# The second head's operands move over by one block, so that the states and the removed values of both heads lie on a diagonal and one masked VectorE operation keeps them

## The chip, the cores and the metric

The kernel runs on one core of a Trainium2 chip. Five engines take part: TensorE (PE, its weight loads shown apart as PEld), VectorE (DVE), ScalarE (ACT), GpSimd (POOL) and SyncE (SP), which only issues transfers here. Each engine works through its own instructions in the order in which they stand; semaphores hold an instruction until what it needs is there. The metric is device time in microseconds (us), the median of several runs of one program; lower is better.

## The reference, cut to what matters

One decoder layer: an RMSNorm, one input projection, then 16 heads of RWKV-7 time mixing beside 16 heads of dilated window attention, an output projection and a last RMSNorm. The change lies in the time mixing, whose recurrence is, per head with a 64x64 state:

```
def step(state, inp):
    r_t, w_t, k_t, v_t, av_t, bv_t = inp              # av = -kk, bv = kk * a
    sa = jnp.einsum('bhvk,bhk->bhv', state, av_t)     # the value that is removed
    state = (state * w_t[:, :, None, :] + sa[..., None] * bv_t[:, :, None, :]
             + v_t[..., None] * k_t[:, :, None, :])
    return state, jnp.einsum('bhvk,bhk->bhv', state, r_t)
```

SEQ is 1024, the head size 64. All tensors are float32.

## The kernel before

**Units and slots.** The recurrence is computed in blocks of C = 64 steps. Two heads (a pair) share the 128 partitions, one in rows 0 to 63 and one in rows 64 to 127. A unit is one pair and one half of the sequence, so there are 16 units of NC_ = 8 blocks. `rwkv` goes over the units; at each unit it lays the work of four units at different stages into 24 slots: the chain of this unit, `finish` of the one before, `late` and `invert` of the next, `prepare` and `products` of the one after that. Behind the events of a slot it sends 4 matmuls of the input projection (128x512, from `proj_steps`, L179) to TensorE as filler. A scheduler that runs when the program is built may shift instructions a little on each engine, so the built order is what counts.

**The chain** (`chain`, three slots a block, called a step here) is serial. `first`: z = AR·Sd + MV·Vd on TensorE, where Sd [128, 2, 64] holds both heads' states as a block diagonal; `spread` (L704, L705) copies z into zd, again as a block diagonal, DVE the first head's half and ACT the second's. `second`: z = U·zd on TensorE gives the removed values; `spread` (L707 on DVE, L708 on ACT) scales them by rn (DVE) and rn1 (ACT) and writes ud. `third`: T = MV·Vd + AR·Sd + TU·ud; rows 0 to 63 of T are the new states of both heads side by side, rows 64 to 127 their outputs; `spread` scales the states by dec and writes the next Sd. All chain matmuls stand on L693 (`mm`). `heads_out` (L745, ACT) copies the outputs of four blocks from T to Y.

**What feeds the chain.** `prepare` builds AR (three 64-column blocks: identity, receptance, removal key), BK and rn on DVE, with dec on POOL (L435) and ACT (L436) and rn1 on ACT (L464). `products` multiplies AR by BK (pa, L559), masks the result into TU on DVE (L566) and copies it to MV on ACT (L569), where a POOL affine_select (L570) clears the future. `invert` builds U, the inverse of a triangular matrix, with column steps and transposes on DVE, small matmuls on PE and a trip through DRAM. `late` adds the turned keys to TU and MV and the values to Vd.

**Behind the time mixing** the same TensorE queue goes on with the attention and the output projection, which the change does not touch.

Of the kernel before, what the change touches and what calls it, by code (L numbers as in the profile page):

```python
# [45 lines left out]
class Kern:  # L46
# [237 lines left out]
    def rwkv(self, pairs=range(NPAIR), apairs=range(NPAIR)):  # L284
        nc = self.nc
        with ExitStack() as ctx:
# [99 lines left out]
    def prepare(self, d):  # L386
# [66 lines left out]
        def norm():  # L453
# [9 lines left out]
            d["rn1"] = self.mid.tile([64, NC_], F32, name="rn1", bufs=3)  # L463
            S.copy(out=d["rn1"], in_=rn[64:128])  # L464
# [17 lines left out]
        def receptance():  # L482
            V.tensor_tensor(out=self.c192(d["AR"])[:, :, 1], in0=c3(d["rs"]), in1=d["W"][:, :, 1:C + 1], op=ALU.mult)
# [10 lines left out]
    def late(self, d):  # L494
# [28 lines left out]
        def keys2(c4):  # L523
            tq, cs = t["tq"], slice(c4 * 4, c4 * 4 + 4)
            for e in range(2):
                er = slice(e * 64, e * 64 + 64)
                S.copy(out=d["TU"][er, cs, 0], in_=tq[0:64, :, e])
                S.copy(out=self.c192(d["MV"])[er, cs, 0], in_=tq[64:128, :, e])
# [14 lines left out]
    def products(self, d):  # L543
        nc = self.nc
        V, S, G = nc.vector, nc.scalar, nc.gpsimd
        er = [slice(0, 64), slice(64, 128)]

        def step(c4):
# [14 lines left out]
        def step2(c4):  # L563
            cs, q = slice(c4 * 4, c4 * 4 + 4), d["pq"]
            for e in (1, 0):
                V.tensor_tensor(out=d["TU"][er[e], cs, 1:3].rearrange("p c a t -> p c (a t)"), in0=q[e][0:64],  # L566
                                in1=bc(self.mask[0:64, 1].unsqueeze(1), (64, 4, 128)), op=ALU.mult)
                f = self.c192(d["MV"])[er[e], cs, 1:3].rearrange("p c a t -> p c (a t)")
                S.copy(out=f, in_=q[e][64:128])  # L569
                G.affine_select(out=f, in_=f, pattern=[[0, 4], [-1, 2], [1, 64]], compare_op=ALU.is_ge, fill=0.0, base=0,  # L570
                                channel_multiplier=-1)
# [18 lines left out]
    def invert(self, d, U):  # L590
# [17 lines left out]
        def clear():  # L608
            G.memset(U[:, 0:NC_], 0.0)

        def back():
            ud = self.dpool.tile([4, 16, 16, 16], F32, name="ud")
            nc.sync.dma_start(out=ud.rearrange("b q s t -> (b q) (s t)"), in_=d["UB"])
            for e in range(2):
                for b in range(4):
                    r = e * 64 + b * 16
                    nc.sync.dma_start(out=U[r:r + 16, 0:NC_, b * 16:b * 16 + 16],
# [6 lines left out]
        def m0():  # L624
            t["UT"] = self.tmp("vr2", "UT", (128, NC_, C))
            t["Xs"] = self.inv.tile([128, NC_, 32], F32, name="Xs")
            V.transpose(out=fl(t["UT"]), in_=fl(U[:, 0:NC_]))

        def m1():
            xq = t["xq"] = self.ps_tr.tile([128, NC_, 16], F32, name="xq", tag="tr")  # L630
            for c in range(NC_):
                for g in range(4):
                    b = 32 * (g % 2)
                    nc.tensor.matmul(xq[hs(g), c], lhsT=t["LT"][rs(g), c, b:b + 16], rhs=U[rs(g), c, b + 16:b + 32], start=True,
# [6 lines left out]
        def m2():  # L641
            dq = t["dq"] = self.ps_tr.tile([128, NC_, 16], F32, name="dq", tag="tr")
            for c in range(NC_):
                for g in range(4):
                    b = 32 * (g % 2)
                    nc.tensor.matmul(dq[hs(g), c], lhsT=t["UT"][hs(g), c, b:b + 16], rhs=t["Xs"][hs(g), c, 0:16], start=True,
                                     stop=True, skip_group_check=True)

        def m2c():
            for g in range(4):  # L650
                b = 32 * (g % 2)
                S.copy(out=U[hs(g), 0:NC_, b + 16:b + 32], in_=t["dq"][hs(g)])
# [6 lines left out]
        def m3():  # L659
            x2 = t["x2"] = self.ps_tr.tile([128, NC_, 32], F32, name="x2", tag="tr")  # L660
            for c in range(NC_):
                for e in range(2):
                    nc.tensor.matmul(x2[hi[e], c], lhsT=d["TU"][lo[e], c, 2, 32:64], rhs=t["UT"][lo[e], c, 0:32], start=True,
# [20 lines left out]
    def chain(self, d, nxt):  # L684

# [15 lines left out]
        def spread(out, q, scale):  # L701

            if scale is None:
                V.tensor_copy(out=out[er[0], 0], in_=q[0:64, 0:64])  # L704
                S.copy(out=out[er[1], 1], in_=q[0:64, 64:128])  # L705
            else:
                V.tensor_scalar(out=out[er[0], 0], in0=q[0:64, 0:64], scalar1=scale[0], scalar2=None, op0=ALU.mult)  # L707
                S.activation(out=out[er[1], 1], in_=q[0:64, 64:128], func=AF.Copy, scale=scale[1])  # L708

        def first(c):  # L710
# [7 lines left out]
            spread(zd, t["z"][:, 0], None)  # L718
# [3 lines left out]
        def second(c):  # L722
            mm(t["z"][0:66, 1], f2(d["U"])[:, c * 64:c * 64 + 66], self.zds[c % 2], True, True)
            spread(self.uds[c % 2], t["z"][:, 1], [d["rn"][0:64, c:c + 1], d["rn1"][:, c:c + 1]])

        def third(c):
# [8 lines left out]
            spread(self.Sds[(c + 1) % 2], T, [dec[:, e, n:n + 1] for e in range(2)])  # L735
# [4 lines left out]
    def heads_out(self, d, c4):  # L740
# [3 lines left out]
        for e in range(2):  # L744
            self.nc.scalar.copy(out=d["Y"][e * 64:e * 64 + 64, 4 * c4:4 * c4 + 4], in_=d["T", c4][64:128, :, e * 64:e * 64 + 64])  # L745
# [418 lines left out]
```

## Time and profile before

| what | value |
|---|---|
| median of 3 runs | 1553.68 us (1553.39 to 1553.86) |
| profiled execution, its own time | 1555.3 us |
| its span, first to last instruction | 1553.6 us |
| mean granted TensorE clock over the span | 0.998 of full speed (2.4 GHz) |
| matmul instructions | 10721 |
| chain of the first unit starts, chain of the last ends | about 114 us, about 842 us |

The profiled execution is one run with the hardware profiler on. A busy time is the sum over an engine's instructions without overlaps. Matmuls are pipelined: one 128x512 matmul is shown as about 0.40 us long while the next starts 0.23 us after it, so that a short wait of TensorE hides in the tail of the matmul ahead of it and the busy share of PE looks better than it is. "Idle before" is the time in which an engine had nothing running just before an instruction, and the arrow names what ended it.

### The profile page before, as it was taken

To read this page: it belongs to the slowest core of one execution; us is meant where nothing else is said; L and a number is where in the kernel's file an instruction comes from. 1 tells how busy PE (TensorE), PEld (TensorE's weight loads), DVE (VectorE), ACT (ScalarE), POOL (GpSimd) and SP (SyncE) were. 2 spreads that over 40 slices of the span, in tenths; PEclk is the share of its full clock that TensorE was granted. 3 is DMA by queue.
4 is the path that set the end of the run, shared out by engine and by line. 5 is a ranking of instruction groups with operands and counts; after the bars stand their busy time and mean duration, and the time that the engine had idled before them with its cause. 6 is when DMAs were issued, how large, how long until landed. Compare 5 with 4: busy or idle time off the path is not lost.

```text
span 1553.6 us, 29135 instructions
## 1 busy us (share of the span) xinstructions
PE 1486.1 (96%) x10721; PEld 1201.3 (77%) x10721; DVE 1009.3 (65%) x2776; ACT 897.6 (58%) x2080; POOL 442.0 (28%) x563
## 2 busy tenths in 40 slices
PE   5999999999999999999999999999999999899997
PEld 4877777777777777777777788888888888787886
DVE  6866776667776677766743557667676666956144
ACT  6655666666676666666643556555565565655221
POOL 3211111111111121112211534334443343456442
PEclk9999999999999999999999999999999999999999
DMA  6321111111111111111111201111111111426452
GB/s 199 90 48 33 41 40 39 41 34 40 47 32 41 47 33 41 39 38 41 34 39 34 70 28 42 35 35 34 38 52 34 36 55 55 159 92 203 142 161 99
DMA packets 178829, 94.87 MB, mean 61 GB/s; under 512 B 58413, under 2 KB 164606, under 8 KB 178686
## 3 DMA queue, kind: packets, MB, share of 16 engines
q1 hardware_dynamic: 174942, 86.19, 19.4%
q10 hardware_dynamic: 3744, 6.82, 1.3%
q8 instruction: 84, 1.38, 0.4%
q14 instruction: 59, 0.48, 0.1%
HBM read 75.01 MB, written 17.83 MB: 60 GB/s over the span
## 4 chain that ended last, share of the span: by engine, by line
PE 60%; DVE 17%; ACT 16%; issue 3%; DMA 2%; POOL 1%; SPq 0%; DVEq 0%; ACTq 0%; POOLq 0%
PE pq L179 28%; PE oq L1048 10%; PE o L994 3%; PE z L693 3%; PE T L693 3%; PE mp L921 2%; PE sp L954 2%; ACT Y L745 1%; DVE I L422 1%; ACT MV L569 1%; PE sp L974 1%; ACT Vd L513 1%; DVE TB L604 1%; ACT shtmp L213 1%; PE pa L559 1%
## 5 line engine op out<-in xcount | busy, mean ns | idle before, releaser
L179 PE MATMUL pq<-xh,wh 128*128 128x512 f32 x1040 | 429.1, 413 | 0.0
L179 PE MATMUL pq<-xl,wh 128*128 128x512 f32 x1040 | 412.3, 396 | 0.0
L179 PE MATMUL pq<-xh,wl 128*128 128x512 f32 x1040 | 303.3, 409 | 0.0
L179 PEld LDWEIGHTS pq<-xh,wh 128*128 128x128 f32 x1040 | 195.9, 188 | 32.6 <-ACT xh L157 0.3
L179 PEld LDWEIGHTS pq<-xl,wh 128*128 128x128 f32 x1040 | 196.4, 189 | 30.9 <-DVE xl L158 0.4
L179 PEld LDWEIGHTS pq<-xh,wl 128*128 128x128 f32 x1040 | 184.5, 189 | 31.9
L1048 PE MATMUL oq<-ow,qr 128*128 128x512 f32 x512 | 161.9, 394 | 1.2 <-ACT ow L1029 0.6
L982 POOL TENSOR_TENSOR pl<-p,ph 128x512 fp32r<-128x512 f32 (+2 forms) x96 | 102.3, 1072 | 202.2 <-ACT ph L981 182.4
L923 DVE CUSTOM_DVE_ANT_0 mp<-mp,maskq 128x512 f32<-128x512 f32 (+1 forms) x192 | 105.5, 570 | 68.4 <-PE mp L921 59.9
L977 ACT ACTIVATE p<-p 128x512 f32<-128x512 f32 (+2 forms) x144 | 64.6, 452 | 104.2 <-DVE p L976 103.3
L171 POOL TENSOR_TENSOR wl<-wraw,wh 128x512 fp32r<-128x512 f32 x64 | 85.5, 1354 | 110.4 <-PE pq L179 58.4
L1043 POOL TENSOR_TENSOR vr<-kr,qr 128x512 fp32r<-128x512 f32 (+2 forms) x68 | 90.8, 1340 | 80.5 <-ACT qr L1042 70.0
L1048 PEld LDWEIGHTS oq<-ow,qr 128*128 128x128 f32 x512 | 95.9, 188 | 22.8 <-ACT ow L1029 1.1
L1048 PE MATMUL oq<-ow,vr 128*128 128x512 f32 x256 | 101.2, 395 | 1.9 <-POOL vr L1043 1.9
L170 ACT CAST wh<-wraw 128x512 fp32r<-128x512 f32 x138 | 80.7, 616 | 28.6 <-PE pq L179 23.4
L1042 ACT CAST qr<-kr 128x512 fp32r<-128x512 f32 (+2 forms) x68 | 40.2, 594 | 93.5 <-PE oq L1048 52.0
L976 DVE TENSOR_TENSOR p<-sp,maskt 128x512 f32<-128x512 f32 (+2 forms) x144 | 65.2, 457 | 43.3 <-PE sp L974 41.9
L570 POOL TENSOR_SCALAR_AFFINE_SELECT MV<-MV 64x512 f32<-64x512 f32 x64 | 47.8, 747 | 125.2 <-ACT MV L569 114.2
L708 ACT ACTIVATE ud<-z,rn 64x64 f32<-64x64 f32 x128 | 39.3, 307 | 65.3 <-DVE ud L707 63.6
L707 DVE TENSOR_SCALAR ud<-z,rn 64x64 f32<-64x64 f32 x128 | 34.3, 268 | 58.1 <-PE z L693 57.9
L693 PEld LDWEIGHTS T<-ud,TU 128*128 128x128 f32 x256 | 42.5, 188 | 34.8 <-ACT ud L708 28.2
L708 ACT ACTIVATE Sd<-T,dec 64x64 f32<-64x64 f32 x120 | 36.9, 307 | 53.5 <-DVE Sd L707 52.0
(236 smaller groups left out, 3158.4 us busy)
## 6 DMA issues: line engine op xcount, KB each, us to landing
wraw<-in_w_in_dram SPq DMA_DIRECT2D x138, 256.0 KB
kr<-mixd SPq DMA_DIRECT2D x60, 256.0 KB
oraw<-in_w_out_dram SPq DMA_DIRECT2D x16, 512.0 KB
xt<-in_x_dram SPq DMA_DIRECT2D x8, 512.0 KB
ld<-TU SPq DMA_DIRECT2D x32, 128.0 KB
mixd<-zt SPq DMA_DIRECT2D x16, 256.0 KB
mixd<-gt SPq DMA_DIRECT2D x16, 256.0 KB
xr<-in_x_dram ACTq DMA_DIRECT2D x16, 256.0 KB
```

What stands on the lines that cost most here:

```text
L170: nc.scalar.copy(out=wh[:, ks], in_=raw)
L171: eng.tensor_tensor(out=wl[:, ks], in0=raw, in1=wh[:, ks].bitcast(F32), op=ALU.subtract)
L179: return [lambda i=i, a=a, b=b: self.nc.tensor.matmul(q, lhsT=a, rhs=b, start=(i == 0), stop=(i == len(ops) - 1)) for i, (a, b) in enumera ...
L570: G.affine_select(out=f, in_=f, pattern=[[0, 4], [-1, 2], [1, 64]], compare_op=ALU.is_ge, fill=0.0, base=0, channel_multiplier=-1)
L693: mm = lambda out, w, x, start, stop: nc.tensor.matmul(out, lhsT=w, rhs=f2(x), start=start, stop=stop, skip_group_check=True)
L708: S.activation(out=out[er[1], 1], in_=q[0:64, 64:128], func=AF.Copy, scale=scale[1])
L923: V.tensor_tensor_reduce(out=mp[:, :kn], in0=mp[:, :kn], in1=self.maskq[:, v0:v0 + kn], op0=ALU.add, op1=ALU.max, scale=1.0, scalar=-3e38, ...
L976: V.tensor_tensor(out=p[:, :qn], in0=sp[:, :qn], in1=self.maskt[:, u0:u0 + qn], op=ALU.add)
L977: S.activation(out=p[:, :qn], in_=p[:, :qn], func=AF.Exp)
L982: G.tensor_tensor(out=pl[:, :qn], in0=p[:, :qn], in1=ph[:, :qn].bitcast(F32), op=ALU.subtract)
L1043: nc.gpsimd.tensor_tensor(out=ml, in0=raw, in1=mh.bitcast(F32), op=ALU.subtract)
L1048: nc.tensor.matmul(q, lhsT=m[:, i], rhs=v, start=(k == 0 and j == 0), stop=(k == 15 and j == 2))
```

## The change: what it does, and the diff

For the second head (rows 64 to 127) the blocks of the operands stand one block further or in another order. AR holds [receptance, identity, removal key] there in place of [identity, receptance, removal key], and TU and MV are laid out likewise (`ra` lists the two blocks that `products` writes: 1 and 2 for the first head, 0 and 2 for the second). U stands one block to the right, so U is cleared and transposed over 9 blocks. With that, T and the second z carry the first head's states or removed values in rows 0 to 63 and columns 0 to 63, and the second head's in rows 64 to 127 and columns 64 to 127; what lies off the diagonal is outputs or of no use. `spread` becomes one DVE operation over 128x128: (q times a per-row scale) times the 0/1 block mask `bd`. The first z keeps its two copies. dec becomes one [128, 8] tile written by POOL; rn1 goes. The receptance is written by two half-height DVE operations, the affine_select runs once for each of the two blocks.

```
-            d["dec"] = self.mid.tile([64, 2, NC_], F32, name="dec", bufs=3)
-            G.tensor_copy(out=d["dec"][:, 0], in_=Ux[0:64, :, 0])
-            S.copy(out=d["dec"][:, 1], in_=Ux[64:128, :, 0])
+            d["dec"] = self.mid.tile([128, NC_], F32, name="dec", bufs=3)
+            G.tensor_copy(out=d["dec"], in_=Ux[:, :, 0])
...
-            d["rn1"] = self.mid.tile([64, NC_], F32, name="rn1", bufs=3)
-            S.copy(out=d["rn1"], in_=rn[64:128])
...
-            V.tensor_tensor(out=self.c192(d["AR"])[:, :, 1], in0=c3(d["rs"]), in1=d["W"][:, :, 1:C + 1], op=ALU.mult)
+            for e in range(2):
+                er = slice(e * 64, e * 64 + 64)
+                V.tensor_tensor(out=self.c192(d["AR"])[er, :, 1 - e], in0=c3(d["rs"])[er], in1=d["W"][er, :, 1:C + 1],
+                                op=ALU.mult)
...
+        ra = [slice(1, 3), slice(0, 3, 2)]
...
-                    nc.tensor.matmul(q[e][:, b], lhsT=BK[er[e], c], rhs=AR[er[e], c * 192 + 64:c * 192 + 192], start=True,
+                    nc.tensor.matmul(at(q[e][:, b]), lhsT=BK[er[e], c], rhs=self.c192(AR)[er[e], c, ra[e]], start=True,
                                      stop=True)
...
-                G.affine_select(out=f, in_=f, pattern=[[0, 4], [-1, 2], [1, 64]], compare_op=ALU.is_ge, fill=0.0, base=0,
-                                channel_multiplier=-1)
+                for j in range(2):
+                    G.affine_select(out=f[:, :, j], in_=f[:, :, j], pattern=[[0, 4], [1, 64]], compare_op=ALU.is_ge, fill=0.0,
+                                    base=-j, channel_multiplier=-1)
...
-            t["UT"] = self.tmp("vr2", "UT", (128, NC_, C))
+            t["UT"] = self.tmp("vr2", "UT", (128, NC_ + 1, C))
...
-            V.transpose(out=fl(t["UT"]), in_=fl(U[:, 0:NC_]))
+            V.transpose(out=fl(t["UT"]), in_=fl(U))
...
-            if scale is None:
-                V.tensor_copy(out=out[er[0], 0], in_=q[0:64, 0:64])
-                S.copy(out=out[er[1], 1], in_=q[0:64, 64:128])
-            else:
-                V.tensor_scalar(out=out[er[0], 0], in0=q[0:64, 0:64], scalar1=scale[0], scalar2=None, op0=ALU.mult)
-                S.activation(out=out[er[1], 1], in_=q[0:64, 64:128], func=AF.Copy, scale=scale[1])
+            V.scalar_tensor_tensor(out=f2(out), in0=q, scalar=scale, in1=self.bd, op0=ALU.mult, op1=ALU.mult)
...
-            mm(t["z"][0:66, 1], f2(d["U"])[:, c * 64:c * 64 + 66], self.zds[c % 2], True, True)
-            spread(self.uds[c % 2], t["z"][:, 1], [d["rn"][0:64, c:c + 1], d["rn1"][:, c:c + 1]])
+            mm(t["z"][:, 1], f2(d["U"])[:, c * 64:c * 64 + 128], self.zds[c % 2], True, True)
+            spread(self.uds[c % 2], t["z"][:, 1], d["rn"][:, c:c + 1])
...
-            self.nc.scalar.copy(out=d["Y"][e * 64:e * 64 + 64, 4 * c4:4 * c4 + 4], in_=d["T", c4][64:128, :, e * 64:e * 64 + 64])
+            self.nc.scalar.copy(out=d["Y"][e * 64:e * 64 + 64, 4 * c4:4 * c4 + 4], in_=d["T", c4][64 - e * 64:128 - e * 64, :, e * 64:e * 64 + 64])
```

The order on TensorE stays the same but for small exchanges. On ScalarE, in the fourth step of a unit of the first few pairs, around the copies of the turned values into Vd (L513), before:

```order
L705 COPY zd_127<-z 64x64
L433 ACTIVATE Ux<-I 128x520
L513 COPY Vd_121<-vq 64x4x64 x4
L436 COPY dec<-Ux 64x8
L438 ACTIVATE a<-ta,hk 128x512
L170 CAST wh<-wraw 128x512
L708 ACTIVATE ud_129<-z,rn_3728 64x64
L170 CAST wh<-wraw 128x512
L708 ACTIVATE Sd_122<-T_4766,dec 64x64
L213 ACTIVATE shtmp<-pq,prm 128x512
L705 COPY zd_126<-z 64x64
```

and the same place in the changed kernel (its lines are numbered a little differently: L437 is L438, L719 is L705):

```order
L719 COPY zd_127<-z 64x64
L433 ACTIVATE Ux<-I 128x520
L513 COPY Vd_121<-vq 64x4x64 x4
L437 ACTIVATE a<-ta,hk 128x512
L170 CAST wh<-wraw 128x512 x2
L213 ACTIVATE shtmp<-pq,prm 128x512
L719 COPY zd_126<-z 64x64
```

The two chain operations ud and Sd are gone from between the casts and copies; only zd is left. On VectorE, in the same step and the next, from the removal key (AR<-ks) to the second zd, before:

```order
L469 SCALAR_TENSOR_TENSOR AR_144<-ks,prm,W 128x8x64
L604 TENSOR_TENSOR TB<-UB,AB 64x39
L472 SCALAR_TENSOR_TENSOR BK<-ta,Ux 128x8x64
L606 TENSOR_TENSOR UB<-UB,TB 64x13x3
L476 SCALAR_TENSOR_TENSOR BK<-ks,prm,BK 128x8x64
L604 TENSOR_TENSOR TB<-UB,AB 64x28
L707 TENSOR_SCALAR ud_129<-z,rn 64x64
L606 TENSOR_TENSOR UB<-UB,TB 64x14x2
L477 TENSOR_TENSOR ks<-ks,a 128x512
L604 TENSOR_TENSOR TB<-UB,AB 64x15
L539 TENSOR_TENSOR bv<-bq,vs_4170 128x512
L606 TENSOR_TENSOR UB<-UB,TB 64x15
```

and the same stretch of the changed kernel (L466, L469, L473 are L469, L472, L476 of before; L708 is the new `spread`):

```order
L466 SCALAR_TENSOR_TENSOR AR_143<-ks,prm,W 128x8x64
L608 TENSOR_TENSOR TB<-UB,AB 64x28
L469 SCALAR_TENSOR_TENSOR BK<-ta,Ux 128x8x64
L610 TENSOR_TENSOR UB<-UB,TB 64x14x2
L708 SCALAR_TENSOR_TENSOR ud_129<-z,rn,bd 128x128
L608 TENSOR_TENSOR TB<-UB,AB 64x15
L473 SCALAR_TENSOR_TENSOR BK<-ks,prm,BK 128x8x64
L610 TENSOR_TENSOR UB<-UB,TB 64x15
L708 SCALAR_TENSOR_TENSOR Sd_122<-T_2401,dec,bd 128x128
L474 TENSOR_TENSOR ks<-ks,a 128x512
L539 TENSOR_TENSOR bv<-bq,vs_1818 128x512
L171 TENSOR_TENSOR wl<-wraw,wh 128x512
```

The chain's ud and Sd now stand ahead of one or two of the 128x512 operations of `prepare` that they stood behind.

## Rows read from the trace of the kernel before

**Rows 1.** The page, part 1: busy time, share and instructions by engine.

```profile
PE 1486.1 (96%) x10721; PEld 1201.3 (77%) x10721; DVE 1009.3 (65%) x2776; ACT 897.6 (58%) x2080; POOL 442.0 (28%) x563
```

**Rows 2.** Windows: chain's stage; columns stretch, length, busy PE, PEld, DVE, ACT, POOL.

```profile
114.00:842.00 728.00, 700.45 (x6722) 545.35 (x6721) 490.90 (x1614) 458.71 (x1200) 117.91 (x229) 1.00 0.15 39
```

**Rows 3.** Windows: two units, each cut into steps 1-4 and 5-8.

```profile
395.18:418.77 23.59, 21.88 (x128) 16.98 (x127) 21.52 (x85) 16.84 (x42) 1.76 (x4) 1.00 0.13 37
418.77:442.36 23.59, 23.43 (x319) 18.51 (x318) 11.62 (x25) 13.11 (x36) 5.67 (x12) 1.00 0.19 43
442.36:466.60 24.24, 22.80 (x129) 17.34 (x127) 22.27 (x85) 18.13 (x47) 2.38 (x4) 1.00 0.13 39
466.60:489.70 23.10, 22.92 (x315) 18.14 (x316) 11.14 (x25) 13.43 (x36) 5.74 (x12) 1.00 0.18 41
```

**Rows 4.** Waits, whole span: who waited for whom, us, times, longest.

```profile
ACT ud L708 <- DVE ud L707: 63.6, 64, 1.6
ACT Sd L708 <- DVE Sd L707: 52.0, 66, 1.8
...
PE T L693 <- ACT ud L708: 8.9, 15, 1.3
...
PE z L693 <- ACT Sd L708: 3.8, 19, 0.5
...
PEld T L693 <- ACT ud L708: 28.2, 56, 1.8
PEld z L693 <- ACT Sd L708: 24.3, 48, 0.9
PEld z L693 <- ACT zd L705: 14.8, 26, 0.9
...
PEld bq L533 <- ACT Vd L513: 11.9, 15, 1.9
```

**Rows 5.** Timeline around one wait: start, length, instruction, idle before it.

```profile
400.18 0.28 DVE L707 TENSOR_SCALAR Sd<-T,dec 64x64 f32<-64x64 f32 x1 [0.19 <-PE T L693]
...
400.67 0.40 PE L179 MATMUL pq<-xh,wh 128*128 128x512 f32 x1
...
400.90 0.40 PE L179 MATMUL pq<-xl,wh 128*128 128x512 f32 x1
...
401.15 0.31 ACT L708 ACTIVATE Sd<-T,dec 64x64 f32<-64x64 f32 x1
...
401.51 0.20 PEld L693 LDWEIGHTS z<-Sd,AR 128*66 128x66 f32 x2 [0.65 <-ACT Sd L708]
401.51 0.43 PE L693 MATMUL z<-Sd,AR 128*66 128x128 f32 x2 [0.21 <-ACT Sd L708]
```

**Rows 6.** Lines by shape, VectorE, 0 to 860 us: busy us, mean ns.

```profile
L707 DVE TENSOR_SCALAR ud<-z,rn 64x64 f32<-64x64 f32 x128 | 34.3, 268 | 58.1 <-PE z L693 57.9
...
L422 DVE TENSOR_TENSOR_SCAN I<-d,lw 128x130 f32<-128x130 f32 x64 | 27.8, 439 | 0.0
...
L216 DVE SCALAR_TENSOR_TENSOR rs<-pq,om,shtmp 128x512 f32<-128x512 f32 x16 | 12.0, 750 | 0.7
...
L483 DVE TENSOR_TENSOR AR<-rs,W 128x512 f32<-128x512 f32 x16 | 10.8, 676 | 0.0
```

**Rows 7.** Lines by shape, ScalarE, 0 to 860 us.

```profile
L708 ACT ACTIVATE ud<-z,rn 64x64 f32<-64x64 f32 x128 | 39.3, 307 | 65.3 <-DVE ud L707 63.6
```

**Rows 8.** Lines by shape, TensorE and its weight loads, 114 to 842 us.

```profile
L693 PE MATMUL T<-ud,TU 128*128 128x128 f32 x254 | 54.9, 298 | 10.0 <-ACT ud L708 8.9
...
L693 PE MATMUL T<-Vd,MV 128*128 128x128 f32 x256 | 49.6, 275 | 0.0
```

**Rows 9.** Lines by shape, GpSimd, 0 to 860 us.

```profile
L570 POOL TENSOR_SCALAR_AFFINE_SELECT MV<-MV 64x512 f32<-64x512 f32 x64 | 47.8, 747 | 125.2 <-ACT MV L569 114.2 <-DVE vs L216 5.0 <-DVE ks L216 4.0
```

**Rows 10.** Instructions of L559 and L954: count, min/median/max ns.

```profile
L559 PEld LDWEIGHTS pa<-AR,BK x512: 182/188/188, 63.1 to 759.7; 64*128 64x128 f32 x171
L559 PE MATMUL pa<-AR,BK x512: 272/272/374, 63.1 to 759.8; 64*128 64x128 f32 x171
...
L954 PE MATMUL sp<-Q,KS x64: 278/415/463, 893.0 to 1386.1; 128*128 128x128 f32 x64
```

More of the change, by code (lines that the diff above doesn't have):

```diff
@@ L526, in keys2 @@
                 er = slice(e * 64, e * 64 + 64)
-                S.copy(out=d["TU"][er, cs, 0], in_=tq[0:64, :, e])
-                S.copy(out=self.c192(d["MV"])[er, cs, 0], in_=tq[64:128, :, e])
+                S.copy(out=d["TU"][er, cs, e], in_=tq[0:64, :, e])
+                S.copy(out=self.c192(d["MV"])[er, cs, e], in_=tq[64:128, :, e])
         def bonus():
@@ L608, in clear @@
         def clear():
-            G.memset(U[:, 0:NC_], 0.0)
+            G.memset(U, 0.0)
         def back():
@@ L616, in back @@
                     r = e * 64 + b * 16
-                    nc.sync.dma_start(out=U[r:r + 16, 0:NC_, b * 16:b * 16 + 16],
+                    nc.sync.dma_start(out=U[r:r + 16, e:NC_ + e, b * 16:b * 16 + 16],
                                       in_=ud[b, 8 * e:8 * e + 8].rearrange("q s t -> s q t"))
@@ L633, in m1 @@
                     b = 32 * (g % 2)
-                    nc.tensor.matmul(xq[hs(g), c], lhsT=t["LT"][rs(g), c, b:b + 16], rhs=U[rs(g), c, b + 16:b + 32], start=True,
+                    nc.tensor.matmul(xq[hs(g), c], lhsT=t["LT"][rs(g), c, b:b + 16], rhs=U[rs(g), c + g // 2, b + 16:b + 32], start=True,
                                      stop=True, skip_group_check=True)
@@ L645, in m2 @@
                     b = 32 * (g % 2)
-                    nc.tensor.matmul(dq[hs(g), c], lhsT=t["UT"][hs(g), c, b:b + 16], rhs=t["Xs"][hs(g), c, 0:16], start=True,
+                    nc.tensor.matmul(dq[hs(g), c], lhsT=t["UT"][hs(g), c + g // 2, b:b + 16], rhs=t["Xs"][hs(g), c, 0:16], start=True,
                                      stop=True, skip_group_check=True)
@@ L651, in m2c @@
                 b = 32 * (g % 2)
-                S.copy(out=U[hs(g), 0:NC_, b + 16:b + 32], in_=t["dq"][hs(g)])
+                S.copy(out=U[hs(g), g // 2:NC_ + g // 2, b + 16:b + 32], in_=t["dq"][hs(g)])
         def m2t():
-            V.transpose(out=fl(t["UT"]), in_=fl(U[:, 0:NC_]))
+            V.transpose(out=fl(t["UT"]), in_=fl(U))
         lo = [slice(e * 64, e * 64 + 32) for e in range(2)]
@@ L662, in m3 @@
                 for e in range(2):
-                    nc.tensor.matmul(x2[hi[e], c], lhsT=d["TU"][lo[e], c, 2, 32:64], rhs=t["UT"][lo[e], c, 0:32], start=True,
+                    nc.tensor.matmul(x2[hi[e], c], lhsT=d["TU"][lo[e], c, 2, 32:64], rhs=t["UT"][lo[e], c + e, 0:32], start=True,
                                      stop=True, skip_group_check=True)
@@ L673, in m4 @@
                 for e in range(2):
-                    nc.tensor.matmul(x2[lo[e], c], lhsT=t["Xs"][hi[e], c], rhs=U[hi[e], c, 32:64], start=True, stop=True,
+                    nc.tensor.matmul(x2[lo[e], c], lhsT=t["Xs"][hi[e], c], rhs=U[hi[e], c + e, 32:64], start=True, stop=True,
                                      skip_group_check=True)
@@ L678, in m4c @@
             for e in range(2):
-                S.copy(out=U[lo[e], 0:NC_, 32:64], in_=t["x2"][lo[e]])
+                S.copy(out=U[lo[e], e:NC_ + e, 32:64], in_=t["x2"][lo[e]])
         return [(COLS[j], lambda j=j: column(j)) for j in range(15)] + [
@@ L717, in first @@
             mm(t["z"][0:66, 0], AR[:, c * 192 + 128:c * 192 + 194], Sd, False, True)
-            spread(zd, t["z"][:, 0], None)
+            V.tensor_copy(out=zd[er[0], 0], in_=t["z"][0:64, 0, 0:64])
+            S.copy(out=zd[er[1], 1], in_=t["z"][0:64, 0, 64:128])
             mm(T, d["MV"][:, c * 192:c * 192 + 128], d["Vd"][:, c], True, False)
@@ L734, in third @@
             dec, n = (nxt["dec"], 0) if c == NC_ - 1 else (d["dec"], c + 1)
-            spread(self.Sds[(c + 1) % 2], T, [dec[:, e, n:n + 1] for e in range(2)])
+            spread(self.Sds[(c + 1) % 2], T, dec[:, n:n + 1])
             if n:
```

12 lines of the change are left out of this document (7 added, 5 removed).

## The prediction

> **What bounds the kernel now.** I read the page's busy times first, then windows by stage and by half unit, then the waits, then one wait in the timeline. TensorE is busy 1486.1 of 1553.6 us [rows 1], so the first guess is that nothing on VectorE or ScalarE can matter. In the chain's stage, though, 728.0 us hold 700.5 us of busy PE [rows 2], and that flatters it. In the timeline two filler matmuls start 0.23 us apart (400.67, 400.90) while each is shown 0.40 us long, so the next could have started at 401.13; the chain's matmul started at 401.51. That wait cost 0.38 us, of which the matmul row shows 0.21 and the weight load's row 0.65 [rows 5]. So a wait really costs the matmul row's idle time plus about 0.17 us, or the weight load's less about 0.27.
>
> What TensorE waits for here is the chain, by name: the ACT halves of ud and Sd [rows 4]. And ACT's half is late because it comes second: it waited for DVE's half 64 times (63.6 us) on ud and 66 times (52.0 us) on Sd [rows 4], though the two write different partitions. So each of these two spreads costs one DVE operation (268 ns [rows 6]), then one ACT operation (307 ns [rows 7]), then about 0.05 us until the weight load; where ACT has other work in between it is worse: in the timeline DVE is done at 400.46 and ACT starts at 401.15 [rows 5].
>
> The second thing to see is where in a unit this happens. Both units in the windows are cut after the fourth step. The first halves have 21.88 and 22.80 us of busy PE in 23.59 and 24.24 us, the second halves 23.43 and 22.92 in 23.59 and 23.10. DVE is busy 21.52 and 22.27 us in the first halves, 11.62 and 11.14 in the second [rows 3]. So nearly all the visible idle time lies where DVE is over 90% busy, and the change takes work off ACT and puts it on DVE.
>
> **What goes.** 128 ud and 120 Sd operations of ACT, at 307 ns [rows 7], 76 us of ACT time, none of it on the path by itself but as the last link of a wait. The waits: 56 + 48 = 104, with 28.2 + 24.3 = 52.5 us of idle weight loads, and 8.9 + 3.8 = 12.7 us of idle matmuls [rows 4]. By the timeline's terms the loss is 12.7 + 104 x 0.17 = 30.4 us, or 52.5 - 104 x 0.27 = 24.4 us; I take 27, with 12.7 and 52.5 as the ends. After a wait the second weight load of the pair is not hidden either: T<-ud matmuls take 298 ns where T<-Vd take 275 [rows 8], 254 x 23 ns = 5.8 us; I take 3 of it, since the modelled ends overlap (ends 0 and 6). Do these waits end altogether? The new operation is one DVE scalar_tensor_tensor over 128x128. Its price is not in the trace. Below it stands the 64x64 tensor_scalar with 268 ns, above it the 128x130 scan with 439; a line through 268 ns at 64 columns and the scalar_tensor_tensor's 750 ns at 512 [rows 6] gives 1.08 ns a column and 337 ns. I take 0.34 us. In the timeline's case the path would be 400.18 + 0.34 + 0.05 = 400.57, before TensorE is ready at 401.13. In the shortest case (ACT directly behind DVE) 0.27 + 0.31 becomes 0.34, 0.24 us less, against a mean loss of 27 / 104 = 0.26 us. So with DVE starting when it starts now, close to all of it goes: 30 us.
>
> ACT's shorter queue helps others behind it. The bonus matmul bq waits for ACT's copies of Vd 15 times, 11.9 us of its weight load [rows 4]. The order shows ud and Sd gone from around these copies, but the copies themselves stay where they are, so I count 2 us (ends 0 and 8).
>
> **What it costs.** (1) DVE. Per unit 16 operations grow by 0.34 - 0.27 = 0.07 us (1.1 us), the receptance becomes two operations of the same 512 columns (a second 0.68 [rows 6]), and the transposes of U grow by an eighth: about 1.9 us a unit, of which roughly 1.0 to 1.3 lands in the first half. There DVE has 23.59 - 21.52 = 2.07 and 24.24 - 22.27 = 1.97 us left [rows 3]. What should go from a first half is about 1.5 of the 1.9 us that 30 us make per unit. So demand (1.5) meets what is left of the room (0.7 to 1.0). The order softens this: ud and Sd now stand ahead of one or two 128x512 operations of `prepare` that they stood behind, which moves some of DVE's work into the second half, where half of DVE's time is free. I let a third of a us per unit be lost, 5 us in all; the ends are 0 (the moved work makes room) and 25 (DVE sets the pace of every first half, and only the second halves' part comes through).
>
> (2) zd keeps its two engines. Its 26 waits, 14.8 us [rows 4], stay, and a fuller DVE starts its copy later: 0.07 us more in front of each makes 26 x 0.07 = 2 us. The U matmul loads 128 columns in place of 66; a 128-column load costs 188 ns [rows 10], and even if the 66 columns cost nothing that is hidden behind the filler unless TensorE has just waited, so at most 26 x 2 x 0.19 = 10 us; I take 2, since only the difference counts. Together 4 us (ends 0 and 20).
>
> (3) The affine_select: 64 of 747 ns [rows 9] become 128 over half the columns. Between half the price each and the full price that is 0 to 47.8 us more on POOL, over 728 us in which POOL is busy 117.9 [rows 2]. MV is needed a whole unit later (about 47 us [rows 3]), which hides it. If POOL's small carry copies behind it came late, DVE's token shift would wait, in the second half, where DVE has room. I cost it at nothing.
>
> (4) The U memset grows by an eighth, off the path. The receptance's matmul partners run some slots later; the order puts the pair ahead of them still. The pa matmuls of the second head read two runs of 64 columns that don't touch; the runs are long, so I cost that at nothing, and give the other end below as a rival.
>
> (5) The copies of T to Y now read rows 0 to 63 for the second head, the rows that DVE's Sd reads too. The profile already shows ACT waiting for DVE where both read one z tile [rows 4]. The Trainium skill ("PSUM — Partial Sum Buffer", PSUM bank collisions raise a hardware error) says that engines have to be kept apart per bank and group of 32 partitions, two reads included; by that a Y copy behind the last Sd of a unit would wait for it where it didn't before, 16 x (0.34 + 0.05) = 6 us of ACT time and perhaps 3 us of the end; the trace agrees for z, and no row shows it for Y. I leave it out of the sum, since ACT has just been given 76 us.
>
> **Sum.** 27 + 3 + 2 - 5 - 4 = 23 us. Against the profiled execution's own 1555.3 us that is 1532.3; the median of the runs lies 1.6 us lower (1553.68), so 1530.7, about 1531. By the ends of the terms alone: best 52.5 + 6 + 8 = 66 us (too much, since the weight loads' idle time counts prefetch time as loss), worst 12.7 - 25 - 20 = -32.
>
> **The rivals.**
> *All of it comes.* If the order moves enough DVE work out of the first halves, (1) and (2) cost nothing and bq gains fully: 27 + 6 + 8 = 41 us, 1513. For it: DVE's free half. Against it: over 90% busy in the first halves.
> *DVE becomes the wait.* The first halves don't get shorter, because every us that TensorE stops waiting for ACT it waits for DVE; only the second halves' part of about 0.4 us a unit comes, 6 us, less 4 for zd: 1552, no change that a measurement shows. For it: 21.5 of 23.6 us busy. Against it: the room of 2 us a unit, and that ud and Sd move forward in DVE's order.
> *Slower: the split operand slows the pa matmuls.* The second head's share is 256 matmul instructions of 272 ns. A nearby row in which TensorE reads operands with gaps (every fourth element) has 415 ns [rows 10]. If two runs with a gap cost the same, 256 x 0.143 = 36.6 us are added and the end is 1531 + 37 = 1568, or some 14 us slower than before. It decides from 23 / 256 = 0.09 us an instruction. Against it: the gap comes once in 64 columns, not at each. The Trainium skill ("PSUM — Partial Sum Buffer", Specifications) has a sentence that any non-contiguous access pattern slows matmuls significantly; it speaks of the output in PSUM, which stays contiguous here, and by its widest reading the time is the same 1568; the rows here show it for element gaps alone.
> *The change doesn't do what it says* would be a Sd or ud that still waits for ACT; the order has none, so I give it nothing.
>
> **How the numbers follow.** Forecast 0.64, with its own range of 1520 to 1544; all of it 0.14; DVE becomes the wait 0.15; slower 0.07. A measurement here tells about 0.2%, 3 us, from no change. The forecast and the second case are faster (0.78), the third is half within 3 us and half faster by a little: faster 0.85, same 0.08, slower 0.07. The range takes the likely part of the first rival and most of the third: 1513 to 1550.
>
> **What would show it.** Right: no ACT line among the releasers of T<-ud and z<-Sd; DVE's operation at 0.33 to 0.36 us; their waits below 10 us of weight loads in place of 52.5; first halves of a unit about 1 us shorter, DVE in them above 95%; zd's wait grown a little. Wrong: first halves as long as before with DVE as releaser (second rival); pa matmuls above 272 ns (slower case); or a new long wait for zd. If the spread costs nearer to 0.44 us, the first halves give back 0.8 us a unit, 13 us.

## The result, and the profile after

The changed kernel takes 1518.74 us in the median of four runs (1518.14 to 1519.74), the kernel before 1553.77 us beside it (1553.39 to 1555.29): a ratio of 0.9773, 95% interval 0.9756 to 0.979. The gain is 35.0 us where 23 were forecast. The profiled execution took 1518.14 us, its span is 1516.4 us, and its mean granted TensorE clock 0.995 of full speed (before: 0.998), so the clock has no part in the gain. Of the runs below, one execution of the old layout without small copies is left out: it took 1615.78 us at a mean granted clock of 0.848, the other three 0.994 to 0.999.

The page's busy times:

```profile
PE 1464.4 (97%) x10721; PEld 1212.1 (80%) x10721; DVE 1028.8 (68%) x2792; ACT 811.2 (53%) x1800; POOL 458.1 (30%) x627
```

Against [rows 1] ScalarE has 86.4 us less, in 280 fewer instructions: 248 halves of ud and Sd and 32 small copies (rn1 and half of dec). VectorE has 19.5 us more. The same two units as in [rows 3], cut 0.31 us ahead of the matmul z<-Sd,AR of step 1 and step 5 (columns as in [rows 2], then granted clock, DMA share and GB/s):

```profile
381.10:402.44 21.34, 20.83 (x125) 17.19 (x124) 20.33 (x82) 13.21 (x32) 2.75 (x4) 1.00 0.15 40
402.44:425.72 23.28, 23.28 (x321) 18.91 (x320) 14.09 (x29) 11.28 (x29) 6.43 (x16) 1.00 0.19 42
425.72:447.86 22.14, 21.09 (x125) 17.29 (x123) 20.42 (x82) 13.62 (x36) 1.98 (x4) 1.00 0.15 42
447.86:470.66 22.80, 22.80 (x321) 18.80 (x320) 14.08 (x28) 12.38 (x32) 6.47 (x16) 1.00 0.20 44
```

The two first halves went from 47.83 to 43.48 us, 2.2 us each; the second halves from 46.69 to 46.08, 0.3 each. That is 2.5 us a unit here; 35 us over 16 units are 2.2. The first halves stay nearly full for VectorE (95% and 92%; the prediction had over 95), but they hold *less* of its work (20.3 and 20.4 us for 21.5 and 22.3), and the second halves more (14.1 for 11.6 and 11.1): work moved to where there was room. Most of the gain lies in one place: measured from one z<-Vd,MV matmul to the next, step 4 of the first of these units went from 6.97 to 5.09 us, and the fourth steps of all 16 units together give 25 of the 35 us. The waits, whole span:

```profile
ACT zd L719 <- DVE zd L718: 72.4, 41, 3.8
...
PEld z L698 <- ACT zd L719: 12.8, 30, 1.0
...
PEld T L698 <- DVE ud L708: 12.1, 30, 1.0
...
PEld bq L533 <- ACT Vd L513: 8.4, 9, 2.0
...
PEld z L698 <- DVE Sd L708: 5.3, 22, 0.4
...
PE T L698 <- DVE ud L708: 2.7, 8, 0.6
...
PE z L698 <- ACT zd L719: 1.6, 7, 0.6
```

No ud or Sd waits for ScalarE any more. What was 104 waits of weight loads and 52.5 us [rows 4] is 52 waits and 17.4 us, for VectorE. Groups of lines by shape, up to 840 us:

```profile
L574 POOL TENSOR_SCALAR_AFFINE_SELECT MV<-MV 64x256 f32<-64x256 f32 x128 | 58.2, 477 | 88.2 <-ACT MV L572 69.1 <-DVE TU L569 18.2
L698 PE MATMUL T<-ud,TU 128*128 128x128 f32 x256 | 52.9, 288 | 2.8 <-DVE ud L708 2.7
...
L708 DVE SCALAR_TENSOR_TENSOR ud<-z,rn,bd 128x128 f32<-128x128 f32 x128 | 43.4, 339 | 51.3 <-PE z L698 51.2
...
L708 DVE SCALAR_TENSOR_TENSOR Sd<-T,dec,bd 128x128 f32<-128x128 f32 x120 | 41.3, 344 | 27.3 <-PE T L698 26.3
...
L746 ACT COPY Y<-T 64x256 f32<-64x256 f32 x64 | 23.4, 366 | 43.8 <-PE xq L638 35.4 <-DVE Sd L708 6.1 <-PE T L698 2.0
...
L482 DVE TENSOR_TENSOR AR<-rs,W 64x512 f32<-64x512 f32 x32 | 21.8, 682 | 0.4
```

The masked operation costs 339 and 344 ns (estimate: 0.34 us). And the pa matmuls, of which those of the second head now read two runs with a gap (count, min/median/max ns):

```profile
L562 PE MATMUL pa<-AR,BK x512: 272/272/374, 64.0 to 726.7; 64*128 64x128 f32 x171
```

They cost what they did in [rows 10], and the 256 with the gap have the same mean as the 256 without (288 and 289 ns), so the gap is free here.

### The profile page after: what moved, and what is told of

Its sections match the earlier page's. It is cut to its first block, busy times and chain, and to the rows that moved or that the text cites. A ratio compares the mean times of both kernels' runs of the same rounds, so it can differ in the third digit from the quotient of the medians.

```text
span 1516.4 us, 29032 instructions
## 1 busy us (share of the span) xinstructions
PE 1464.4 (97%) x10721; PEld 1212.1 (80%) x10721; DVE 1028.8 (68%) x2792; ACT 811.2 (53%) x1800; POOL 458.1 (30%) x627
## 4 chain that ended last, share of the span: by engine, by line
PE 71%; DVE 18%; ACT 5%; issue 3%; DMA 2%; POOL 1%; SPq 0%; DVEq 0%; ACTq 0%; POOLq 0%
PE pq L179 35%; PE oq L1049 10%; PE z L698 4%; PE T L698 4%; PE o L995 3%; PE pa L562 2%; PE mp L922 2%; PE sp L955 2%; DVE I L422 1%; DVE UB L610 1%; DVE TB L608 1%; PE sp L975 1%; PE sp L974 1%; DVE wl L171 1%; PE xq L638 1%
## 5 line engine op out<-in xcount | busy, mean ns | idle before, releaser
L179 PE MATMUL pq<-xh,wl 128*128 128x512 f32 x1040 | 296.7, 406 | 0.0
L170 ACT CAST wh<-wraw 128x512 fp32r<-128x512 f32 x138 | 80.1, 615 | 30.2 <-PE pq L179 26.5
L574 POOL TENSOR_SCALAR_AFFINE_SELECT MV<-MV 64x256 f32<-64x256 f32 x128 | 58.2, 477 | 88.2 <-ACT MV L572 69.1
L708 DVE SCALAR_TENSOR_TENSOR ud<-z,rn,bd 128x128 f32<-128x128 f32 x128 | 43.4, 339 | 51.3 <-PE z L698 51.2
L719 ACT COPY zd<-z 64x64 f32<-64x64 f32 x128 | 26.0, 203 | 75.2 <-DVE zd L718 72.4
L922 PE MATMUL mp<-KS,Q 128*128 128x512 f32 (+1 forms) x192 | 60.7, 374 | 2.0 <-DVE mx L924 1.9
L698 PEld LDWEIGHTS z<-zd,U 128*128 128x128 f32 x256 | 45.3, 188 | 21.6 <-ACT zd L719 12.8
```

Source lines behind the costliest of these rows:

```text
L170: nc.scalar.copy(out=wh[:, ks], in_=raw)
L179: return [lambda i=i, a=a, b=b: self.nc.tensor.matmul(q, lhsT=a, rhs=b, start=(i == 0), stop=(i == len(ops) - 1)) for i, (a, b) in enumera ...
L574: G.affine_select(out=f[:, :, j], in_=f[:, :, j], pattern=[[0, 4], [1, 64]], compare_op=ALU.is_ge, fill=0.0, base=-j, channel_multiplier=-1)
L698: mm = lambda out, w, x, start, stop: nc.tensor.matmul(out, lhsT=w, rhs=f2(x), start=start, stop=stop, skip_group_check=True)
L922: nc.tensor.matmul(mp[:, :kn], lhsT=Q1[:, n * 128:(n + 1) * 128], rhs=KS[:, k0:k0 + kn], start=True, stop=True)
```

## The experiments

"Gain" is the time of the kernel before, measured in the same comparison (1553.7 to 1554.8 us), less the median of the run. The changed kernel's own gain is 35.0. The scheduler builds every edited kernel anew, so a difference between two runs can hold, beside the edit, another order of instructions on the engines.

### Which part of the change earns it

**The layout with two engines.** The changed layout, with ScalarE doing the second half of ud and Sd again, now from rows 64 to 127 of z and T:

```
+ V.tensor_scalar(out=out[er[0], 0], in0=q[0:64, 0:64], scalar1=scale[0:64], ...)
+ S.activation(out=out[er[1], 1], in_=q[64:128, 64:128], func=AF.Copy, scale=scale[64:128])
- V.scalar_tensor_tensor(out=f2(out), in0=q, scalar=scale, in1=self.bd, ...)
```

> The changed layout throughout, but ud and Sd written again by two operations: VectorE the first head's diagonal block (rows 0 to 63), ScalarE the second head's (rows 64 to 127). In the built order ScalarE's half still waits for VectorE's. Theory A (the link from VectorE to ScalarE is what the change takes away; the layout itself brings nothing and costs its few extra VectorE operations): 1550 to 1562 us, weight loads of T<-ud and z<-Sd idle for ScalarE about 50 us again. Theory B (the gain comes from the new places of VectorE's other work in the built order and from the layout, not from the link): 1518 to 1535 us.

1542.36 us, ratio 0.9922 (0.9907 to 0.9937), gain 11.4: between the two theories. The link through ScalarE is back as it was in [rows 4]:

```profile
ACT ud L709 <- DVE ud L708: 71.1, 63, 2.0
...
ACT Sd L709 <- DVE Sd L708: 40.3, 52, 1.6
...
PEld T L698 <- ACT ud L709: 26.3, 56, 1.6
...
PEld z L698 <- ACT Sd L709: 17.8, 45, 0.6
```

So 23.6 us of the change hang on taking ScalarE out of ud and Sd (20 of them lie in the fourth steps), and 11 us came from something else in the change: what is left are the 32 small copies, the layout and the built order.

**The small copies.** The kernel before, with the dec half and rn1 copied by GpSimd in place of ScalarE, and nothing else:

```
- S.copy(out=d["dec"][:, 1], in_=Ux[64:128, :, 0])
+ G.tensor_copy(out=d["dec"][:, 1], in_=Ux[64:128, :, 0])
...
- S.copy(out=d["rn1"], in_=rn[64:128])
+ G.tensor_copy(out=d["rn1"], in_=rn[64:128])
```

> The kernel before, with only the 32 small ScalarE copies (half of dec, rn1) moved to GpSimd, as the change drops them from ScalarE. It asks where the 11 us come from by which the changed layout with two engines was faster than the kernel before. If from these copies (200 ns each, each waiting for another engine at the head of ScalarE's queue): 1540 to 1548 us. If from the layout or the built order: 1552 to 1556 us.

1541.10 us, ratio 0.9914 (0.9899 to 0.9928), gain 13.7. (The run before this one has the new layout and two engines; it gained 11.4, so the layout by itself earns nothing that these runs show.) With rn1 alone moved:

> The kernel before with only rn1's 16 copies on GpSimd; dec's half stays on ScalarE. Both together gave 13 us. If dec's copy, which stands between the copies of Vd and ud in the longest step, is what cost: 1551 to 1554 us. If rn1's, which waits for VectorE at the head of ScalarE's queue (3.8 us, 7 times): 1541 to 1546 us.

1543.28 us, ratio 0.9928 (0.9913 to 0.9943), gain 11.2. So moving 16 copies of 0.2 us, 3.1 us of work, is worth 11. The timeline of the kernel before shows how a part of it comes, in the third step of the first unit of [rows 3] (start, length, instruction, idle before it):

```profile
405.40 0.37 ACT L786 COPY zt<-yq 64x256 f32<-64x256 f32 x1
406.00 0.20 ACT L464 COPY rn<-rn 64x8 f32<-64x8 f32 x1 [0.23 <-DVE rn L462]
406.20 1.12 ACT L786 COPY zt<-yq 64x256 f32<-64x256 f32 x3
407.35 0.69 ACT L213 ACTIVATE shtmp<-pq,prm 128x512 f32<-128x512 f32 x1
408.06 0.20 ACT L705 COPY zd<-z 64x64 f32<-64x64 f32 x1
```

The copy stands between the zt copies and waits for VectorE's reciprocal; three zt copies, shtmp and the chain's zd stand behind it, and z<-zd started only at 408.32. In the run with both copies gone the four zt copies go through in one piece, and zd starts 2.24 us behind the first of them for 2.66:

```profile
399.60 1.50 ACT L786 COPY zt<-yq 64x256 f32<-64x256 f32 x4
401.13 0.69 ACT L213 ACTIVATE shtmp<-pq,prm 128x512 f32<-128x512 f32 x1
401.84 0.20 ACT L705 COPY zd<-z 64x64 f32<-64x64 f32 x1
```

That is 0.42 us in this unit, and over 16 units at most 7 us, not 11. Where the rest lies is read from the z<-Vd,MV matmuls of the two units of [rows 3], at the start of steps 3 and 4 and of the next unit, in the kernel before:

```profile
404.49 0.38 PE L693 MATMUL z<-Vd,MV 128*66 128x128 f32 x2
410.66 0.38 PE L693 MATMUL z<-Vd,MV 128*66 128x128 f32 x2
442.12 0.38 PE L693 MATMUL z<-Vd,MV 128*66 128x128 f32 x2
...
450.85 0.38 PE L693 MATMUL z<-Vd,MV 128*66 128x128 f32 x2
457.65 0.38 PE L693 MATMUL z<-Vd,MV 128*66 128x128 f32 x2
489.58 0.38 PE L693 MATMUL z<-Vd,MV 128*66 128x128 f32 x2
```

and with rn1's copy moved:

```profile
399.93 0.38 PE L693 MATMUL z<-Vd,MV 128*66 128x128 f32 x2
405.70 0.38 PE L693 MATMUL z<-Vd,MV 128*66 128x128 f32 x2
437.20 0.38 PE L693 MATMUL z<-Vd,MV 128*66 128x128 f32 x2
...
445.91 0.38 PE L693 MATMUL z<-Vd,MV 128*66 128x128 f32 x2
452.51 0.38 PE L693 MATMUL z<-Vd,MV 128*66 128x128 f32 x2
483.20 0.38 PE L693 MATMUL z<-Vd,MV 128*66 128x128 f32 x2
```

In the first unit step 3 takes 5.77 us for 6.17, about the copy and its wait, and steps 4 to 8 take what they took (31.50 and 31.46); TensorE, VectorE and ScalarE have the same order there but for the copy. In the second unit step 3 gains 0.20 us, and steps 4 to 8 gain 1.24, with another order on all three engines: the receptance AR<-rs,W, for one, starts at 457.83, in step 4, where it started at 468.64, in step 5. Over all units the third steps give 4.0 us. So the copy's delay is worth about 4 us; the other 7 came with a new built order, mainly in every second unit, and whether that order could be had with the copy in place was not tried.

**rn1's copy put back into the changed kernel**, where in the built order it stands behind the second of the four zt copies in one unit and ahead of all four in the next:

```
+ d["rn1"] = self.mid.tile([64, NC_], F32, name="rn1", bufs=3)
+ S.copy(out=d["rn1"], in_=rn[64:128])
```

> The changed kernel with the 16 copies of rn's upper half put back on ScalarE (0.2 us each, 3.1 us in all; nobody reads them). In ScalarE's order each stands where it stood in the kernel before: after the first of the zt copies, ahead of the second zt copy, shtmp and the chain's zd copy, and it still has to wait for VectorE's reciprocal of rn. Theory A (the copy's place in the queue is what costs, and its going is a third of the gain): some 11 us come back, 1526 to 1533 us, the zq matmul's wait for zt and z's wait for zd grow, and step 4 of a unit is longer by 0.5 us or more. Theory B (the copy hurt only together with ScalarE's halves of ud and Sd in the same queue; with those gone the queue catches up): 1517 to 1523 us. In B the 11 us of the earlier run and the 24 us of the halves would not simply add.

1523.58 us, ratio 0.9802 (0.9788 to 0.9815), gain 31.0: between the two theories, nearer to B. The copy still waits for VectorE (where it stands ahead of zt, mostly in time that ScalarE would have waited anyway: its wait for zt's yq goes from 43.0 to 13.8 us), and z's wait for zd grows from 12.8 to 21.0 us, while bq's for Vd falls from 8.4 to 2.4. Of its waits:

```profile
ACT rn L463 <- DVE rn L461: 34.6, 10, 4.4
...
PEld z L700 <- ACT zd L721: 21.0, 39, 1.0
```

The third steps of all units are 4.4 us longer than in the changed kernel, the other steps together 0.8. So the copy costs about 4 us here too. Taken out first, the copy is worth 11; put back last, 4. What differs is not the copy's own delay, which is about the same, but what else the built order does.

**Old layout, both halves on VectorE** (two operations of 64x64 in place of one of 128x128; the copies stay):

```
- S.activation(out=out[er[1], 1], in_=q[0:64, 64:128], func=AF.Copy, scale=scale[1])
+ V.tensor_scalar(out=out[er[1], 1], in0=q[0:64, 64:128], scalar1=scale[1], scalar2=None, op0=ALU.mult)
```

> The layout of the kernel before, with both halves of ud and Sd on VectorE, one 64x64 operation after the other. Theory A (link to ScalarE): most of the gain without any shift of the operands; two operations of about 270 ns that follow each other at some 200 ns make the path about 0.13 us longer than the one masked operation, and VectorE has about 25 us more to do, so 1518 to 1532 us. Theory B (the diagonal layout is needed): 1545 to 1560 us. The waits for zd should be as in the kernel before.

1533.72 us, ratio 0.9868 (0.9853 to 0.9883), gain 20.0. The same with the small copies on GpSimd:

> The layout of the kernel before, both halves of ud and Sd on VectorE as in the earlier run, and in addition the 32 small copies of dec and rn1 on GpSimd: nothing of the chain's ud and Sd on ScalarE, no small copies there, and no shift of the operands. If the layout earns only by making one VectorE operation out of two (and pays its side costs), 1518 to 1528 us; if the small copies' gain adds up fully to that of the earlier run, 1520 us. If the layout itself is needed: 1530 us and more, as in the earlier run (1533.7).

1529.87 us, ratio 0.9841 (0.9822 to 0.9861), gain 24.6. Of the 4.6 us between these two runs 4.3 lie in the third steps; their orders are nearly alike but for the copies, a third time that rn1's copy shows about 4 us. And 10.4 of the 35 us need the diagonal, that is the one operation in place of two: VectorE is busy 1074.2 us here, 45.4 more than in the changed kernel (at the 0.21 us for each that is found below, an estimate of 9.5 us). The waits of this last run say where:

```profile
PEld z L693 <- ACT zd L705: 19.8, 42, 1.3
...
PEld T L693 <- DVE ud L708: 16.1, 37, 0.8
PEld z L693 <- DVE Sd L708: 16.0, 48, 2.2
```

52 us there, 30.2 us in the changed kernel.

### Is it ScalarE's time or its place in the path, and what does VectorE's time cost?

**Loads that nothing ties down.** The changed kernel with one more independent operation for each spread, on ScalarE (64x64; `pad` is a tile that nobody reads):

```
+ S.activation(out=self.pad[0:64, 0:64], in_=self.ident[0:64, 0:64], func=AF.Copy, scale=self.bd[0:64, 0:1])
```

> The changed kernel with one ScalarE operation of 64x64 behind each masked operation, for which nothing waits (it writes a tile that nobody reads): ScalarE is about as loaded as before, and off the chain in ud and Sd. Theory A1 (the link alone counts): at most 3 us slower than the changed kernel, 1518 to 1522 us. Theory A2 (ScalarE's shorter queue is a good part of the gain, through zd, bq and the copies that VectorE and TensorE wait for): 1526 to 1540 us.

and on VectorE (128x96, from constants likewise):

> The changed kernel with one more VectorE operation of 128x96 (about 0.3 us) behind each masked operation, for which nothing waits (it writes a tile that nobody reads): 248 x 0.3 = 75 us more work on VectorE, 4.8 us a unit, half of it in steps 1 to 4. Theory C (steps 1 to 4 are bound by VectorE's work, as the prediction's cost for VectorE had it): 30 to 45 us slower than the changed kernel, 1550 to 1563 us. Theory D (VectorE's other work slides into the later steps, where VectorE has time, and only the places right ahead of zd, ud and Sd count): 3 to 15 us slower, 1522 to 1534 us.

1536.29 us (0.9887, 0.9873 to 0.9902) and 1536.37 us (0.9884, 0.9867 to 0.99). Neither tells anything on the question. What depends on nothing is built in at the program's start: a window there, first of the run with ScalarE's load, columns as in [rows 2]:

```profile
80.00:100.00 20.00, 17.52 (x73) 13.64 (x72) 15.65 (x51) 18.57 (x48) 1.82 (x4) 0.91 0.11 31
```

and of the changed kernel:

```profile
80.00:100.00 20.00, 18.43 (x93) 14.67 (x92) 18.55 (x58) 9.55 (x19) 2.05 (x5) 1.00 0.18 50
```

ScalarE is full (18.57 for 9.55 us), and the first chain starts late (its first z matmul at 121.6 us for 114.1). So the loads were tied to the chain: each reads the spread's output, and nobody waits for it.

```
+ S.activation(out=self.pad[0:64, 0:64], in_=out[er[0], 0], func=AF.Copy, scale=scale[0:64])
```

> The changed kernel with a ScalarE operation of 64x64 that reads what each masked operation has just written and writes a tile that nobody reads, so that it stands in ScalarE's queue where ScalarE's half stood before, waits for VectorE as that did, and nobody waits for it. Link theory (ScalarE's half was a link): at most 4 us slower than the changed kernel, 1518 to 1523 us. Queue theory (what stands behind it on ScalarE paid for it: zd, the copies for bq, Y): 1526 to 1540 us, with longer waits for zd and bq.

1521.39 us, ratio 0.9783 (0.9767 to 0.98), gain 33.4. The page has ScalarE at 883.8 us, 72.6 more than in the changed kernel, nearly what the change took from it, and it costs some 2 us. Each of the first twelve units takes as long as in the changed kernel, within 0.11 us; what is lost lies in the last four. So ScalarE's time by itself is cheap.

```
+ V.scalar_tensor_tensor(out=self.pad, in0=f2(out)[:, 0:96], scalar=scale, in1=self.bd[:, 0:96], ...)
```

> The changed kernel with one more VectorE operation of 128x96 that reads what each masked operation has just written and writes a tile that nobody reads: 75 us more VectorE work, bound to the chain's steps, unlike in the run in which it had drifted to the start of the program. If steps 1 to 4 are bound by VectorE, about half of the 4.8 us a unit shows: 1545 to 1565 us. If VectorE's other work slides into the later steps: 1521 to 1535 us.

1533.35 us, ratio 0.9864 (0.985 to 0.9879), gain 21.4. The page has VectorE at 1093.5 us, 64.7 more, for 13.6 us of the gain: 0.21 us for each, where these operations stand (a mean: about half of the loss lies in the last three units). VectorE is dear, but far from one for one.

### Two attempts to go further

**Both copies of zd on VectorE**, so that no part of the chain is ScalarE's (`S.copy` to `V.tensor_copy` at L719):

> The changed kernel with both copies of zd on VectorE, so that no chain operation is left on ScalarE. Link theory: zd's wait for ScalarE (weight loads idle 12.8 us, 30 times, in the changed kernel) ends as those of ud and Sd did, at the price of 128 x 0.21 us on VectorE: 1508 to 1516 us. Load theory (VectorE is close to its limit in steps 1 to 4, and a second copy in front of z pays for the link): 1517 to 1528 us.

1525.29 us, ratio 0.9812 (0.9797 to 0.9827), gain 29.5: 5.5 us worse than the change. The link that goes is replaced by a second operation on VectorE:

```profile
PEld T L698 <- DVE ud L708: 17.9, 42, 1.4
...
PEld z L698 <- DVE zd L719: 13.6, 32, 1.0
...
PEld yq L779 <- DVE Y L773: 12.8, 15, 2.2
```

z still waits 13.6 us for zd (12.8 with two engines), ud's wait grows from 12.1 to 17.9, and yq's for Y from 6.5 to 12.8.

**The receptance on GpSimd** (L482, `V.` to `G.`), to take 22 us off VectorE:

> A version meant to beat both: the changed kernel with the two halves of the receptance on GpSimd in place of VectorE. VectorE loses 32 operations of 0.68 us (21.8 us); by the run with 75 us more VectorE work behind the chain (14.6 us slower) a us of VectorE work is worth about 0.19 us, so 4 us less: 1513 to 1517 us. GpSimd's multiplications are longer; if the receptance comes too late for the pa matmuls, or its work holds up VectorE: 1519 to 1530 us.

1566.41 us, ratio 1.0074 (1.0059 to 1.0089): slower than before the change. GpSimd takes twice as long for it,

```profile
L482 POOL TENSOR_TENSOR AR<-rs,W 64x512 f32<-64x512 f32 x32 | 43.3, 1354 | 53.5 <-ACT W L428 37.1 <-DVE UB L610 15.2
```

and while it runs, VectorE's operations take longer. In one unit of this run,

```profile
421.69 1.77 DVE L466 SCALAR_TENSOR_TENSOR AR<-ks,prm,W 128x512 f32<-128x512 f32 x1
421.73 2.77 POOL L482 TENSOR_TENSOR AR<-rs,W 64x512 f32<-64x512 f32 x2 [2.79 <-ACT W L428]
423.39 1.15 DVE L608 TENSOR_TENSOR TB<-UB,AB 64x28 f32<-64x28 f32 x1
```

and at the same place of the changed kernel:

```profile
398.84 0.74 DVE L466 SCALAR_TENSOR_TENSOR AR<-ks,prm,W 128x512 f32<-128x512 f32 x1
399.50 0.17 DVE L608 TENSOR_TENSOR TB<-UB,AB 64x28 f32<-64x28 f32 x1
```

So VectorE's page time grew to 1044.2 us (1028.8 in the changed kernel) though 21.8 us of work had left it, and the chain's ud stands behind it:

```profile
PEld T L698 <- DVE ud L708: 40.3, 26, 2.8
```

The first chain starts 4 us later, and most units are 3 us longer, nearly all of it in steps 4 and 5. The mean granted clock fell too (0.984, 0.97 in the chain's stage, 0.995 in the changed kernel); its part was not told apart.

The changed kernel stays the fastest of all that ran.

## Why the prediction was right, and where it fell short

**The mechanism was right.** ScalarE's halves are gone as releasers, the masked operation costs its 0.34 us, and it is the link, not the engine's time, that counted: with the time back and no link 33.4 of the 35.0 us stay, with the link back 11.4. The time lies just below the forecast's own range (1520 to 1544) and inside the whole one (1513 to 1550). Without the 11.4 us of the run with two engines, for most of which the sum had no term, it would have come out near the 1531 of the forecast, and that is in part luck, since the terms below were off in both directions. One named sign was missed: waits of 17.4 us are left for "below 10".

**The step that was mis-sized: ScalarE's shorter queue.** Under "What goes" it had 2 us (ends 0 and 8), all of it for bq, and the small copies had no term: a 0.2 us copy off the path looked free. bq gave 0.6 to 1.9 us by the prediction's two terms (its weight load waits 8.4 us in 9 times for 11.9 in 15, its matmul 4.9 in 7 for 4.5 in 8). But rn1's copy held zd's queue behind a wait for VectorE, about 4 us in three pairs of runs, and taking both kinds of copies out of the old kernel gave 13.7 with the new built order. The row to look at for the 4 us was in the timeline: not how long the copy takes, but what it waits for and what stands behind it. The rest could be seen only in the built order.

**The waits themselves (27 + 3).** They did not all go: 52 waits and 17.4 us of weight loads are left. By the prediction's own two terms (the matmul row has 2.7 us of them left, all of it for ud) what is left costs 3 us (17.4 - 52 x 0.27) or 12 us (2.7 + 52 x 0.17), so 19 to 21 us of the 24 to 30 came this way. The T<-ud matmuls went from 298 to 288 ns, 2.6 us for the 3 taken. The run with two engines gives 23.6 us for this part. Of the costs only the masked operation's is in it (VectorE 1018.2 us there, 1028.8 in the changed kernel, at 0.21 us for each some 2 us), so what the prediction had for it is 27 + 3 - 2 = 28. The built order differs between these two runs as well; the waits by name account for most of the 23.6 us, and what the order gave or took of it was not told apart.

**Cost (1), VectorE, 5 us.** VectorE grew by 19.5 us on the page (the changed operations alone by 30.7, as the 1.9 us a unit had it); at 0.21 us for each that is an estimate of 4 us, so the size stood. The ends (0 and 25) were a matter of where the work lies, and the prediction's reason for the low side was borne out: the first halves hold 1.2 to 1.9 us less of VectorE's work, the second halves 2.5 to 2.9 more. "DVE becomes the wait" fell with that: the first halves got 2.2 us shorter, twice the 1 us announced.

**Cost (2), zd, 4 us: not there.** z's weight load waits 12.8 us for zd, 14.8 before, and its matmul 1.6 for 4.8; the announced growth did not come. ScalarE is early at its half now and waits there 72.4 us for VectorE's (50.1 before). U's wider load shows a little: 188 ns for 137, and the z<-zd matmuls 283 for 278, 1.3 us.

**Costs (3) and (4): right at nothing.** The affine_select takes 58.2 us for 47.8, and the matmuls T<-Vd,MV have no idle time before them. The pa matmuls stayed at 272 ns: the slower rival, 1568 us, was wrong in its premise. The sentence of the Trainium skill named there ("PSUM — Partial Sum Buffer", Specifications) stands among the properties of PSUM, and its widest reading is refuted for a gap in the operand behind 64 columns; the 415 ns of every fourth element [rows 10] was the wrong neighbour.

**(5), Y behind Sd.** The wait is there: Y waits 6.1 us for DVE's Sd, which it did not before. The Trainium skill's rule on bank collisions ("PSUM — Partial Sum Buffer", PSUM bank collisions raise a hardware error) had asked for it, and the trace agrees. That the 6 us fit is luck: it waited 9 times, 0.7 us each, where 16 times 0.39 were reckoned. What it costs the end was not tried apart; ScalarE's whole 72.6 us came to some 2.

**"All of it comes" (1513)** was the nearest rival: off by 6 on the far side of the result as the forecast is by 12 on the near one. It too lacked the copies, and it counted every wait as gone.

## What to carry to other kernels

For an operation that the change removes or adds, price not its length but its place: what it waits for, and what stands behind it in its queue; a 0.2 us copy with a 0.2 us wait cost the chain 0.4. A value that two engines make half by half cost a link here even where the halves are independent, so one wider operation on one engine can be worth more than the work it adds. And where a scheduler builds the order anew, measure a part both alone in the old kernel and put back into the new one, and compare the built orders step by step, before a difference is put down to the part: of 11 us, 4 were the copy's.

## What the runs showed of the hardware that was not expected

- Two engines on one PSUM tile: with ScalarE reading rows 64 to 127 and VectorE rows 0 to 63 of the same z, ScalarE still waited for VectorE (71.1 us, 63 times). Whether the shared tile or its bank is the reason was not tried apart.
- VectorE slows down beside GpSimd's product of two tensors: its 128x512 operation L466 took 1637 ns in the mean of that run for 744 in the changed kernel, and a 64x28 operation right behind it 1.15 us for 0.17.
- GpSimd needs 1354 ns for a 64x512 product of two float32 tensors in SBUF, VectorE 682; GpSimd's affine_select over 64x256 takes 477 ns, over 64x512 747.
- A matmul operand of two 64-column runs with a gap costs no more than one of 128 columns (272 ns), where an operand of every fourth element had 415 [rows 10].
